# First FFN: down products with the tokens standing, their sums turned by VectorE and read back by GpSimd

## The chip, the cores and the metric

One core of one Trainium2 chip runs the whole kernel. The metric is the device time of one execution in microseconds (us). The engines are TensorE (PE; its weight loads are shown apart as PEld), VectorE (DVE), ScalarE (ACT), GpSimd (POOL) and SyncE (SP). SP and POOL issue the DMAs here: SP's go through hardware queues, POOL's through a software queue.

## The reference

One decoder layer for 512 tokens of 1024 features in float32: an FFN, a mixer of a linear recurrence and windowed attention, and a second FFN, each between two RMS norms, with a residual.

```python
def swiglu(x, w_gu, w_down):
    gate, up = jnp.split(x @ w_gu, 2, axis=-1)
    return (jax.nn.silu(gate) * up) @ w_down
...
x = x + 0.5 * rms_norm(swiglu(rms_norm(x, ffn1_pre_g[l]), ffn1_w_gu[l], ffn1_w_down[l]), ffn1_post_g[l])
```

The hidden width is 2816, or 22 blocks of 128. The case is about the first FFN's `@ w_down`, and about the sum that its post-norm takes over the 1024 features of each token.

## The kernel before

Every product is made of three matmuls on split operands: a high half (`hh`, `whi`, made by ACT's cast) and a low half (`hl`, `wlo`, made by DVE's subtraction), as high by high, low by high and high by low. A matmul has 128 standing columns (its weight load) and up to 512 moving ones.

The first FFN's hidden blocks come in groups (`GROUPS1`): blocks 0 to 3, 4 to 7, 8 to 11, 12 to 15, and 16 to 21.

- **Blocks 0 to 3** (`classic`): gate and up plainly; then the down product of the four blocks, 96 matmuls of 512 columns, chunk by chunk of 128 output features, and each chunk's sum goes to HBM (the loop over `c` with `g == 0`).
- **Groups 4, 8 and 12** run as `octo`: gate and up by a scheme with seven products in place of eight. Their down product (`seven_down`, line 1088) follows while the next octo's forms are made. It has seven steps `a11, s3, a12, s2, s4, a22, s1`, each a product of 256 hidden by 512 outputs by 256 tokens. `by_channels` (L1347) makes a step of 24 matmuls: four blocks of 128 output features stand as weights, 256 tokens move. After six of the steps ACT copies the two PSUM banks to `stage` (L1113), and POOL adds them to the running sums in HBM (`yp_a`, `in_hbm`; accumulating DMAs of L1116). Sums lie there with output features on partitions.
- **Blocks 16 to 21**: an octo of 16 to 19 whose hidden values go through HBM (`h_a`) and come back by SP's reads (`hxa`), then `last_chunks`: blocks 20 and 21 by a smaller scheme (`quad`, L881) whose forms are `u2a` and `g1a`. Then the down product, chunk by chunk: chunks 0 and 1 together, 2, 3 and 4 alone, and chunks 5 to 7 late, in two halves of 256 tokens (`ay`).

At the end each chunk's product is joined with its sum from HBM (`res.chunk` L676, `res.late` L692, both on DVE), squared by ACT, and the squares are added: chunks 0 to 4 by POOL into `acca`, the late halves by DVE into `accb` (L705, L709). PE then takes the mean over features (`rms_r`, L550) of the first 256 tokens, in the middle of the second halves, and of the others after them. The scaled sums are added to x, which POOL reads back from HBM (L1357). `boundary` holds this part.

The next stage's weights (`raw_xl`, `raw_kv`) are loaded by SP through a ring of five `raw` buffers, and `W` hands out units (cast by ACT, low half by DVE) in the order of use. `W.owed` is a list of functions called in place of weight loads.

For the second FFN the seven steps already have tokens as standing operand (`by_tokens`, L1884 to L1886), since its output is wanted with tokens on partitions.

## Time and profile before

| | |
|---|---|
| median of 3 runs | 842.86 us (842.47 to 843.58) |
| the profiled execution | 842.55 us, span 840.8 us |
| PE busy | 832.2 us (99%), 4504 instructions |
| PEld busy | 718.9 us (85%) |
| DVE, ACT, POOL busy | 723.8 (86%), 520.9 (62%), 162.6 us (19%) |
| granted TensorE clock | 0.999 |
| POOL's writes to `yp_a` | 50 of 256 KB, 9.1 us to landing |

A row of the time line has the start, the duration, the engine, the line of the program, the operation, what it writes `<-` reads, the shape and the count; in brackets the idle time before it and what ended it. SPq is SP issuing a DMA: its duration is that of the issue, not of the transfer. A row of the chain of waits has the start, the length, the engine and how many instructions it stands for. Where a part of the span is looked at by itself, the share of busy time over all 840.8 us says little: look at what ends the waits there.

### The profile page before, as it was taken

How to read it: one execution, taken by the hardware profiler on the slowest of the kernel's cores; microseconds unless marked ns; L12 is line 12 of the kernel's file. 1: busy time of each engine (PE TensorE's matmuls, PEld its weight loads, DVE VectorE, ACT ScalarE, POOL GpSimd, SP SyncE). 2: the span in 40 equal slices, each digit the busy share in tenths (PEclk: the TensorE clock that was granted, in tenths of full speed). 3: DMA queues.
4: the chain of work that ended last, by engine and by line, in shares of the span. 5: the costliest groups of instructions: out<-in, count | busy, mean ns of one | idle time of the engine just before them, and what ended most of it. 6: DMA issues, size and time to landing. Idle time of an engine off the chain costs nothing.

```text
span 840.8 us, 12378 instructions
## 1 busy us (share of the span) xinstructions
PE 832.2 (99%) x4504; PEld 718.9 (85%) x4504; DVE 723.8 (86%) x1026; ACT 520.9 (62%) x821; POOL 162.6 (19%) x178
## 2 busy tenths in 40 slices
PE   9999999999999999999999999999999999999996
PEld 8988888988988998987788899888888888888885
DVE  4978999998989965879889589799999899898996
ACT  6646756666666655556797456536758667666562
POOL 2023000140320333304531052002004114032001
PEclk9999999999999999999999999999999999999999
DMA  7249429398595799323511131169439939769842
GB/s 252 77 128 347 135 79 318 80 251 267 123 255 186 167 261 331 93 62 108 157 51 51 51 105 47 50 129 290 179 106 232 317 92 257 253 149 258 305 140 101
DMA packets 123614, 143.73 MB, mean 171 GB/s; under 512 B 23897, under 2 KB 81569, under 8 KB 123041
## 3 DMA queue, kind: packets, MB, share of 16 engines
q1 hardware_dynamic: 109232, 111.86, 42.0%
q0 software_dynamic: 14176, 30.94, 17.0%
q8 instruction: 35, 0.57, 0.3%
q14 instruction: 27, 0.21, 0.1%
q10 hardware_dynamic: 144, 0.13, 0.0%
HBM read 100.45 MB, written 40.89 MB: 168 GB/s over the span
## 4 chain that ended last, share of the span: by engine, by line
PE 96%; DVE 2%; DMA 1%; SPq 0%; issue 0%; ACT 0%; DVEq 0%; ACTq 0%
PE aa L951 10%; PE ab L951 10%; PE db L951 5%; PE da L951 5%; PE yaa L1347 3%; PE bb L951 3%; PE ba L951 3%; PE yda L1347 2%; PE ya L506 2%; PE ya L507 2%; PE ya L508 2%; PE aa L881 1%; PE a_first L1206 1%; PE yab L1884 1%; PE yab L1885 1%; PE yab L1886 1%
## 5 line engine op out<-in xcount | busy, mean ns | idle before, releaser
L1116 POOL DMA_DIRECT2D yp_a<-stage x42 | 36.8, 1064 | 182.6 <-ACT stage L1113 158.8
L1116 POOL DMA_DIRECT2D yp_b<-stage x42 | 36.4, 1084 | 144.3 <-ACT stage L1113 117.8
L506 PE MATMUL ya<-hha,whi_ad 128*128 128x512 f32 x62 | 24.1, 389 | 0.0
L507 PE MATMUL ya<-hla,whi_ad 128*128 128x512 f32 x62 | 24.1, 389 | 0.0
L508 PE MATMUL ya<-hha,wlo_ad 128*128 128x512 f32 x62 | 24.1, 389 | 0.0
L686 POOL TENSOR_TENSOR acca_r<-acca_r,sq_r 128x512 f32<-128x512 f32 x6 | 8.1, 1357 | 61.7 <-ACT sq_r L536 61.7
L1900 POOL DMA_DIRECT2D yp_b<-stage x8 | 4.3, 548 | 67.1 <-ACT stage L1899 67.1
L524 PE MATMUL an<-xh_mx,whi_xl 128*128 128x256 f32 x64 | 15.9, 289 | 0.0
L525 PE MATMUL an<-xh_mx,wlo_xl 128*128 128x256 f32 x64 | 15.5, 283 | 0.0
L2003 POOL TENSOR_TENSOR last<-yp,grow 128x512 f32<-128x512 f32 x3 | 3.9, 1290 | 57.2 <-DVE yp L1993 57.2
L2000 ACT ACTIVATE ysq<-yp 128x512 f32<-128x512 f32 (+1 forms) x8 | 4.8, 606 | 16.2 <-DVE yp L1993 16.2
L506 PE MATMUL gt<-xh_mx,whi_gt 128*128 128x512 f32 x32 | 14.3, 445 | 0.0
L508 PEld LDWEIGHTS ya<-hha,wlo_ad 128*128 128x128 f32 x62 | 11.6, 188 | 2.4
L506 PEld LDWEIGHTS ya<-hha,whi_ad 128*128 128x128 f32 x62 | 11.6, 188 | 2.4
L507 PEld LDWEIGHTS ya<-hla,whi_ad 128*128 128x128 f32 x62 | 11.6, 188 | 2.4
L536 ACT ACTIVATE sq_r<-yp_a 128x256 f32<-128x256 f32 (+1 forms) x10 | 5.0, 502 | 12.9 <-DVE yp_a L676 5.9
L506 PE MATMUL pq<-xh_mx,whi_q 128*128 128x512 f32 x32 | 12.8, 399 | 0.0
L506 PE MATMUL pub<-xh_f,whi_bu 128*128 128x512 f32 x32 | 12.6, 395 | 0.0
L508 PE MATMUL gt<-xh_mx,wlo_gt 128*128 128x512 f32 x32 | 12.6, 394 | 0.0
L506 PE MATMUL pgb<-xh_f,whi_bg 128*128 128x512 f32 x32 | 12.6, 393 | 0.0
L507 PE MATMUL gt<-xl_mx,whi_gt 128*128 128x512 f32 x32 | 12.6, 392 | 0.0
L508 PE MATMUL pgb<-xh_f,wlo_bg 128*128 128x512 f32 x32 | 12.5, 390 | 0.0
(2014 smaller groups left out, 3468.8 us busy)
## 6 DMA issues: line engine op xcount, KB each, us to landing
yp_a<-stage POOLq DMA_DIRECT2D x50, 256.0 KB, 9.1
yp_b<-stage POOLq DMA_DIRECT2D x50, 256.0 KB, 9.0
h_a<-za SPq DMA_DIRECT2D x16, 256.0 KB
hxa<-h_a SPq DMA_DIRECT2D x16, 256.0 KB
h_b<-zb SPq DMA_DIRECT2D x16, 256.0 KB
hxb<-h_b SPq DMA_DIRECT2D x16, 256.0 KB
xn<-in_x SPq DMA_DIRECT2D x8, 256.0 KB
xT_hbm<-xT POOLq DMA_DIRECT2D x2, 1024.0 KB, 9.8
```

Source lines behind the costliest of these rows:

```text
L506: pe.matmul(ps, hi[:, k, :], xh, start=start, stop=False)
L507: pe.matmul(ps, hi[:, k, :], xl, start=False, stop=False)
L508: pe.matmul(ps, lo[:, k, :], xh, start=False, stop=stop)
L524: pe.matmul(ps[:, sl], hi[:, k, :], xh, start=k == 0 and not goes_on, stop=False, skip_group_check=True)
L525: pe.matmul(ps[:, sl], lo[:, k, :], xh, start=False, stop=False, skip_group_check=True)
L881: pe.matmul(o, w[:, k, js], x, start=first and i + j + k == 0, stop=k == 3 and i == 2, skip_group_check=True)
L951: pe.matmul(b[tb], x[:, blk], w[:, k, :], start=first and q + k + j == 0, stop=q + k == 2 and j == 2, skip_group_check=True)
L1116: pool.dma_start(o, st.rearrange("p (a b) -> p a b", a=2) if len(o.shape) == 3 else st, accum_op=ALU.add)
L1206: pe.matmul(banks[j][:, HALF[0]], ws[j][part][:, k, :], n1.xs[k][xpart][:, HALF[0]], start=k == 0 and part == xpart, stop=stop and k == KD ...
L1347: pe.matmul(o, a[:, k, ms], x[:, js], start=first and i + k + m % 2 == 0, stop=k == 1 and i == 2, skip_group_check=True)
L1884: pe.matmul(banks[i], hh[:, js], hi[:, k, :], start=first and k == 0, stop=False, skip_group_check=True)
L1885: pe.matmul(banks[i], hh[:, js], lo[:, k, :], start=False, stop=False, skip_group_check=True)
```

## The change

1. The seven steps of the first FFN's down product take `by_dealt_tokens` in place of `by_channels`: 128 tokens of a hidden block stand, 512 weight columns move, 12 matmuls a step. The hidden halves are kept as four blocks of 64 + 64 tokens in the order in which a later 32x32 turn wants them (`by_blocks`, `dealt`, `in_turn`), and `hxa` comes back in two DMAs in place of four.
2. The sums in HBM are rows: `yr_a`, tokens on partitions, eight pieces of 128x512. The first group's down product (`first_down`) also has tokens standing, in two passes of four banks, with its weights loaded as two raws and made into four units, and the hooks that make the next octo's sums and lows moved with them.
3. The last step (`s1`) of the last octo stays in its two PSUM banks (`hold`), and isn't copied nor added in HBM.
4. At the end of the FFN SP reads the eight row pieces, behind the last weight loads (`W.owed`). DVE turns them in blocks of 32x32 (`turn_sums`), the second half after adding the held banks; SP writes them to `yt_a`, output features on partitions; POOL reads the eight chunks back (`read_sums`).
5. POOL's masks are made earlier, and `decay_factor` moves from the first octo to the second.

```diff
+    def by_token_blocks(o, h, w, k, blk, start, stop):
+        (hh, hl_), (hi, lo) = h, w
+        for j, (x, a) in enumerate(((hh, hi), (hh, lo), (hl_, hi))):
+            pe.matmul(o, x[:, blk], a[:, k, :], start=start and j == 0, stop=stop and j == 2, skip_group_check=True)
+    def by_dealt_tokens(banks, w, h, first):
-    def by_channels(banks, w, h, first):
-        (hi, lo), (hh, hl_) = w, h
-        for m in range(4):
-            o, ms = banks[m // 2][:, HALF[m % 2]], slice(m * P, (m + 1) * P)
+        for i in range(2):
             for k in range(2):
-                js = HALF[k]
-                for i, (a, x) in enumerate(((hi, hh), (hi, hl_), (lo, hh))):
-                    pe.matmul(o, a[:, k, ms], x[:, js], start=first and i + k + m % 2 == 0, stop=k == 1 and i == 2, skip_group_check=True)
+                by_token_blocks(banks[i], h, w, k, slice((2 * i + k) * P, (2 * i + k + 1) * P), first and k == 0, k == 1)
...
+    def read_rows(dh):
+        t = wpool.tile([P, NB * T], F32, tag="raw", name=f"rows_a{dh}", bufs=NRAW)
+        row_sums[dh] = [t[:, tb * T:(tb + 1) * T] for tb in range(NB)]
+        for tb in range(NB):
+            sync.dma_start(row_sums[dh][tb], rows_hbm[tb, dh])
+    def turn_sums(dh):
+        z = wpool.tile([P, NB * T], F32, tag="raw", name="zy1", bufs=NRAW) if dh else wide("zy0")
+        for tb in range(NB):
+            if dh:
+                dve.tensor_add(row_sums[dh][tb], row_sums[dh][tb], held[tb % 2])
+            dve.transpose(z.rearrange("p (j b n) -> p b j n", n=32, b=NB)[:, tb], row_sums[dh][tb].rearrange("p (j n) -> p j n", n=32))
+        for i in range(4):
+            sync.dma_start(turned_hbm[dh][:, i * P:(i + 1) * P].rearrange("(j a) n -> a j n", a=32), z[32 * i:32 * (i + 1)].rearrange("p (j n) -> p j n", n=P))
+    def read_sums(cs):
+        for c in cs:
+            parts[c] = t2k(f"yp_a{c}")
+            pool.dma_start(parts[c], turned_hbm[c // 4][(c % 4) * P:(c % 4 + 1) * P])
...
             if g > 1:
-                seven_down(hid, before, by_channels, lambda half, dh, i: in_hbm[2 * dh + i][:, half], hid.forms, AHEAD - 1)
+                held = seven_down(hid, before, by_dealt_tokens, lambda half, dh, i: rows_hbm[2 * half + i, dh], hid.forms, AHEAD - 1, hold=f1 == FC)[1, 1]
             if f1 == FC:
-                W.owed = [lambda: None] * 2
+                W.owed = [W.load, W.load, lambda: read_rows(0), lambda: read_rows(1)]
+                neg, upf = masks()
...
-            for c in range(5):
-                parts[c] = t2k(f"yp_a{c}")
-                sync.dma_start(in_halves(parts[c]), in_hbm[c // 2][:, :, c % 2])
+        for dh in range(2):
+            turn_sums(dh)
+        dve.tensor_copy(up8f, upf)
+        read_sums(range(4))
```

PE, the first step (`a11`) of the down product of group 4: its first six matmuls before, then after. A row has the line, the bank written, and behind `<-` the moving operand first and the standing one second.

```order
L1347 MATMUL yaa_1627<-hha_1446,whi_adp__1516 128x256
L1347 MATMUL yaa_1627<-hla_1448,whi_adp__1516 128x256
L1347 MATMUL yaa_1627<-hha_1446,wlo_adp__1517 128x256
L1347 MATMUL yaa_1627<-hha_1446,whi_adp__1516 128x256
L1347 MATMUL yaa_1627<-hla_1448,whi_adp__1516 128x256
L1347 MATMUL yaa_1627<-hha_1446,wlo_adp__1517 128x256
```

```order
L1360 MATMUL yaa_1611<-whi_adp__1500,hha_1430 128x512
L1360 MATMUL yaa_1611<-wlo_adp__1501,hha_1430 128x512
L1360 MATMUL yaa_1611<-whi_adp__1500,hla_1432 128x512
L1360 MATMUL yaa_1611<-whi_adp__1500,hha_1430 128x512
L1360 MATMUL yaa_1611<-wlo_adp__1501,hha_1430 128x512
L1360 MATMUL yaa_1611<-whi_adp__1500,hla_1432 128x512
```

Weights and hidden values have changed places, the moving width has doubled, and a step has 12 such rows where it had 24.

SP, at the end of the first FFN, from the last weights of its down product (`raw_ad`) to the first of the next stage, before and after:

```order
L175 DMA raw_ad__3210<-in_ffn_w_down 128x6x256
L175 DMA raw_ad__3281<-in_ffn_w_down 128x6x256
L1380 DMA yp_a_3322<-yp_a_591 128x2x256
L1380 DMA yp_a_3324<-yp_a_591 128x2x256
L1380 DMA yp_a_3326<-yp_a_592 128x2x256
L1380 DMA yp_a_3328<-yp_a_592 128x2x256
L1380 DMA yp_a_3330<-yp_a_593 128x2x256
L1309 DMA gates_raw<-in_w_rg 64x4x64 x2
L1309 DMA gates_raw<-in_w_ig 64x4x64 x2
L175 DMA raw_xl__3349<-in_w_in 128x8x256
L1389 DMA yp_a_3394<-yp_a_593 128x2x256
```

```order
L1376 DMA rows_a_2940<-yr_a_597 128x512
L1376 DMA rows_a_3014<-yr_a_592 128x512
L1376 DMA rows_a_3014<-yr_a_594 128x512
L1376 DMA rows_a_3014<-yr_a_596 128x512
L1376 DMA rows_a_3014<-yr_a_598 128x512
L1385 DMA yt_a_599<-zy_3058 32x16x128 x4
L1385 DMA yt_a_600<-zy_3067 32x16x128 x4
L1332 DMA gates_raw<-in_w_rg 64x4x64 x2
L1332 DMA gates_raw<-in_w_ig 64x4x64 x2
L175 DMA raw_xl__3099<-in_w_in 128x8x256
L175 DMA raw_xl__3192<-in_w_in 128x8x256
L175 DMA raw_kv<-in_w_in 128x8x256
```

The eight reads of ready chunks (the last two of them and raw_xl's second load stand behind the rows shown) have become eight reads of rows (three more stand ahead, behind `raw_ad`) and eight writes of turned sums, all ahead of the gates and of the next weights.

DVE, at the same place, behind the quad's last form, before and after:

```order
L891 TENSOR_TENSOR hla_3077<-g1a_3085,hha_3076 128x2x4x32
L1329 CAST up_590<-upf 128x512
L215 TENSOR_TENSOR wlo_ad_0_3284<-raw_ad__3210,whi_ad_0_3283 128x768
L215 TENSOR_TENSOR wlo_ad_1_3346<-raw_ad__3210,whi_ad_1_3345 128x768
L676 TENSOR_TENSOR yp_a_3322<-ya_3354,yp_a_3322 128x512
L676 TENSOR_TENSOR yp_a_3324<-ya_3355,yp_a_3324 128x512
```

```order
L908 TENSOR_TENSOR hla_2803<-g1a_2811,hha_2802 128x2x4x32
L1383 STREAM_TRANSPOSE zy_3058<-rows_a_2940 128x16x32 x4
L1382 TENSOR_TENSOR rows_a_3014<-rows_a_3014,yaa_2609 128x512
L1383 STREAM_TRANSPOSE zy_3067<-rows_a_3014 128x16x32
L1382 TENSOR_TENSOR rows_a_3014<-rows_a_3014,yaa_2610 128x512
L1383 STREAM_TRANSPOSE zy_3067<-rows_a_3014 128x16x32
L1382 TENSOR_TENSOR rows_a_3014<-rows_a_3014,yaa_2609 128x512
L1383 STREAM_TRANSPOSE zy_3067<-rows_a_3014 128x16x32
L1382 TENSOR_TENSOR rows_a_3014<-rows_a_3014,yaa_2610 128x512
L1383 STREAM_TRANSPOSE zy_3067<-rows_a_3014 128x16x32
L1449 CAST up_590<-upf 128x512
L215 TENSOR_TENSOR wlo_ad_0_3020<-raw_ad__2813,whi_ad_0_3019 128x768
```

Twelve instructions now stand between the last form and the low halves of the weights of chunks 4 to 7; the subtraction of chunk 0 follows two rows further.

## The prediction

> **What bounds the kernel now.** I read the page first: the busy times, then the chain that ended last.

> ```profile
> span 840.8 us, 12378 instructions
> PE 832.2 (99%) x4504; PEld 718.9 (85%) x4504; DVE 723.8 (86%) x1026; ACT 520.9 (62%) x821; POOL 162.6 (19%) x178
> PE 96%; DVE 2%; DMA 1%; SPq 0%; issue 0%; ACT 0%; DVEq 0%; ACTq 0%
> ```

> TensorE (PE) is busy for all but 8.6 us of the span and is 96% of the chain. So there are only two ways to move the time: give PE less to do, or make it wait where it doesn't wait now. The profiled execution took 842.55 us, 1.75 more than its span; the median of the three runs, 842.86, lies 0.31 above it. All sums below are made in the profiled execution, and 0.31 is added at the end. About 0.2% (1.7 us) is what a measurement of this kernel can tell from no change, and the chances are split there.

> Next the chain of waits in order of time, round a down stage of the first FFN, and the table by stretches: its columns are PE busy, weight loads (PEld), DVE, ACT, POOL, granted clock, DMA share, GB/s. The first three stretches are the three down stages of seven steps in the first FFN; the last is the same stage in the second FFN, where the tokens already stand.

> ```profile
> 152.97 2.04 PE aa L951 x9
> 155.01 2.87 PE yaa L1347 x24
> ...
> 172.28 2.88 PE yaa L1347 x24
> 175.16 5.01 PE aa L951 x22
> ```

> ```profile
> 155.01:175.16 20.15, 20.15 (x170) 20.15 (x169) 20.08 (x23) 14.65 (x22) 7.05 (x8) 1.00 0.65 153
> 213.27:233.43 20.16, 20.16 (x170) 20.16 (x169) 19.59 (x22) 14.65 (x22) 6.99 (x8) 1.00 0.66 154
> 271.53:291.69 20.16, 20.16 (x171) 20.16 (x170) 18.50 (x21) 12.47 (x19) 6.72 (x8) 1.00 0.63 142
> 621.92:640.96 19.04, 19.04 (x86) 15.77 (x85) 19.04 (x22) 12.13 (x19) 6.63 (x8) 1.00 0.54 126
> ```

> See two things. A step of 24 matmuls with 256 moving columns takes 2.88 us, 0.120 each, and the weight loads fill the whole stretch: 20.15 of 20.15. In the second FFN the same seven steps are 84 matmuls of 512 columns, 19.04 us, 0.227 each, with 3.3 us of the load path free. The granted clock is 1.00 in all four.

> **The gain.** The first FFN's three stages take the form of the last row: 20.15 + 20.16 + 20.16 - 3 x 19.04 = **3.35 us** less. DVE is full in the fourth row (19.04 of 19.04) and PE still does not wait, so DVE's 20.08 us in the first is no objection: its weights are made steps ahead. [...]

> **The first group.** Its 96 down matmuls keep their number and 512 columns; only the operands change places. Two looser things move: the first weights of the next octo now go ahead of the fourth block's low halves on DVE.

> ```profile
> 72.72 0.69 DVE L659 TENSOR_TENSOR t24l_a<-tb_a,t24h_a 128x512 fp32r<-128x512 f32 x1
> ```

> ```profile
> 78.85 5.44 PE aa L951 x24
> ```

> Those lows end at 73.4 now, and would end near 75 to 76; the first octo product starts at 78.85 and uses the fourth block some 3.6 us into its 24 matmuls. Cover of 6 us: cost zero, and if the cover were gone, at most the 2 us of delay. The strided casts (`by_blocks`, `in_turn`) have the form of the quad's (L891 below, 0.76 for two of 256 columns, against 0.69 for one flat 512): nothing.

> **The end of the FFN.** Here is the price. Today eight chunks come back from HBM long before PE has the products they join. Now rows must be read, turned by DVE, written, and read again by GpSimd, all after the quad's last form. DVE, ACT and SyncE rows of that place now, and PE's:

> ```profile
> 315.53 0.76 DVE L891 TENSOR_TENSOR hla<-g1a,hha 128x256 fp32r<-128x256 f32 x2 [0.47 <-ACT hha L888]
> ...
> 319.39 1.37 DVE L676 TENSOR_TENSOR yp_a<-ya,yp_a 128x512 f32<-128x512 f32 x2 [1.02 <-PE ya L508]
> ...
> 334.64 1.74 DVE L215 TENSOR_TENSOR wlo_xl<-raw_xl__3440,whi_xl 128x1024 fp32r<-128x1024 f32 x1 [0.50 <-ACT whi_xl L210]
> ...
> 339.84 0.43 DVE L709 TENSOR_TENSOR accb_r<-accb_r,sq_r 128x256 f32<-128x256 f32 x1 [0.53 <-ACT sq_r L536]
> ```

> ```profile
> 312.39 0.84 ACT L210 CAST whi_ad<-raw_ad__3210 128x768 fp32r<-128x768 f32 x1 [3.91 <-DMA raw_ad__3210<-in_ffn_w_down]
> ...
> 313.75 0.59 ACT L921 ACTIVATE g1a<-aa 128x512 f32<-128x512 f32 x1
> ...
> 320.75 1.28 ACT L482 ACT_TABLE_LOAD   x1
> ...
> 322.68 0.82 ACT L210 CAST whi_ad<-raw_ad__3281 128x768 fp32r<-128x768 f32 x1
> ```

> ```profile
> 298.37 0.47 SPq L175 DMA_DIRECT2D raw_ad__3210<-in_ffn_w_down  x1
> ...
> 311.03 2.39 SPq L1309 DMA_DIRECT2D gates_raw<-in_w_rg  x2
> 314.27 1.31 SPq L1309 DMA_DIRECT2D gates_raw<-in_w_ig  x2
> ```

> ```profile
> 308.96 2.88 PE aa L881 x24
> 311.85 0.23 PE ya L506
> ...
> 341.99 0.34 PE rms_r L550 x4
> ```

> The residual's mean (L550) is the deadline: it needs the last partial sum (L709), which ends at 340.27, 1.7 us early. With 3.35 us less before it, PE ends the quad at 308.5 and wants that sum at **338.6**. How late the sum comes is worked out hop by hop.

> *Start of the turning.* DVE takes it up after hla of g1a, at 316.29 now. ACT was held there until 312.39 by a load issued at 298.37. Lower end: PE's 308.5 and the 2.5 us from g1a's activation (313.75) to 316.29, so 311.0. Upper end: nothing shifts, 316.3. The load's slot is freed by PE's progress, so it moves with the 3.35; the four accumulating writes that the held step drops (1 MB) relieve the DMA queues somewhat. I take 311.7.

> *Turn, write, land.* Two rows of DVE and SyncE give the same pattern in an octo:

> ```profile
> 159.48 1.30 DVE L961 STREAM_TRANSPOSE za<-g1a 128x512 f32<-128x512 f32 x2
> ```

> ```profile
> 219.07 2.83 SPq L965 DMA_DIRECT2D h_a<-za  x4
> ...
> 224.36 3.27 SPq L1021 DMA_DIRECT2D hxa<-h_a  x4
> ```

> Four turns 2.5, four writes 2.83, and 2.46 more until their reader could be issued (224.36 - 221.90): the first half is in HBM at 319.5.

> *GpSimd's reads.* Software DMAs of 256 KB, from the group's writes, and the times of 1 MB loads:

> ```profile
> L1416 POOL DMA_DIRECT2D yp_a<-stage x8: 682/697/833, 65.5 to 82.8; - x8
> ...
> DMA to landing us min/median/max: 2.5/6.1/8.8
> ```

> ```profile
> L210 ACT CAST whi_bd<-raw_bd x2: 1032/1040/1047, 565.1 to 566.5; 128x1024 fp32r<-128x1024 f32 x2
> ...
> L175 SPq DMA_DIRECT2D raw_bd<-in_ffn_w_down x1: 455/455/455, 559.7 to 559.7; - x1
> ```

> ```profile
> 75.72 1.69 SPq L175 DMA_DIRECT2D raw_ay__901<-in_ffn_w_gu  x2
> ```

> ```profile
> 85.20 1.23 DVE L296 TENSOR_TENSOR raw_ax__862<-raw_ay__901,raw_ax__862 128x1024 f32<-128x1024 f32 x1 [3.12 <-DMA raw_ay__901<-in_ffn_w_gu]
> ```

> A 256 KB read lands 2.5 to 8.8 us after its issue; 4.5, between the least and the median, gives chunk 0 at 324.0. PE has its product by then, so chunk 0's subtraction on DVE now waits for a DMA, and queued behind it are wlo of raw_ad46 (two), the lows of raw_xl and every later sum.

> *The next weights.* raw_xl2's load now takes the buffer of raw_ad46, which is free when DVE has its second low. From chunk 0 (319.39) to the end of that weight's cast (323.50) is 4.1 us on ACT, table load included, and the low adds 0.95: issue at 329.1. A 1 MB load took 5.4 (raw_bd, 559.7 to 565.1) and 9.5 (raw_ay__901, 75.7 to 85.2); with GpSimd's eight reads and raw_xl0 about, 6.5, nearer to the quiet one because those reads are spread over some 10 us: 335.6. Cast 1.04. From the low of raw_xl2 (334.64) to the last sum (340.27) is 5.6. Sum at **342.3**.

> *SyncE's side* agrees. The second half's four sums and four turns take 4.9 more on DVE (319.1), its writes 2.83, the gates 4.55 as now (311.03 to 315.58) and raw_xl0 follows at 326.5; landed at 332 to 333, two casts and lows, chunk 4 and the late halves, some 9.7, end at 342 to 343.

> So PE waits 342.3 - 338.6 = 3.7 us at the mean, once; c5 to c7's second halves follow at their old pace, and x's reload (GpSimd) lands in that wait. Net -3.35 + 3.7 = +0.35, 842.9 for this execution, and 843.2 with the 0.31. The two dropped ACT copies and the fewer hxa issues lie beside PE: nothing.

> **Rivals.**

> *The round trip hides* (faster). For it: the short end of each link, 311.0 + 2.5 + 2.83 + 2.46 + 2.5 = 321.3, then 5.05, a load of 5.4, and 6.65 give 338.4, before 338.6. PE waits for nothing: 842.86 - 3.35 = **839.5**. [...] It decides where the sum comes before 340.2. Against it: the DMA engines are full at this place.

> ```profile
> 309.00:312.00 3.00, 3.00 (x26) 2.96 (x25) 2.97 (x5) 0.00 (x0) 0.00 (x0) 1.00 1.10 234
> ```

> *The hops land as under load* (slower). One mechanism: with the queues full as in that row, GpSimd's reads take their median 6.1 and raw_xl2 its 9.5. That is 1.6 + 3.0 us later: the sum at 346.9, PE waits 8.3, net +5.0, **847.8**; with the turning also at 313.5, 849.6. It decides from a sum at 343.6 on, 1.3 us behind my forecast: the median landing alone suffices.

> [...]

> **How the numbers follow.** The forecast, within 1.7 us of no change: 0.34. The round trip hides by enough: 0.31. Lands late: 0.32; steps don't shorten: 0.03, together 0.35 slower. The likeliest case has 841.2 to 844.5 for its own; the range is 839.4 (all hidden) to 848.5, and leaves out only the last of the loaded case.

> **What would show it.** Steps of 2.72 in the chain at the three stages: the gain. PE's idle before L555's mean (the L550 of now), put down to the sum: the wait; its size says which case. The landing of GpSimd's eight reads, ACT's and DVE's waits for raw_xl: which hop. DVE's first turn before 311 or after 314 would break the start. The prediction falls altogether if PE waits at another place, in the first group for instance.

## The result, and the profile after

The changed kernel takes **854.15 us** (median of four runs, 850.15 to 854.82) against 842.93 for the kernel before on the same chip: 1.0123 times, 95% interval 1.009 to 1.0155. It is slower, and outside the range on record; the forecast was 843.2. The profiled execution took 854.6 us.

The first two lines of the profile's page:

```profile
span 852.5 us, 11869 instructions
PE 834.6 (98%) x4252; PEld 709.1 (83%) x4252; DVE 735.5 (86%) x1034; ACT 519.2 (61%) x815; POOL 159.6 (19%) x182
```

PE has 252 instructions less and yet is busy 2.4 us longer: matmuls got slower somewhere, and PE stood still besides. The 11.7 us between the two spans fall on these places in PE's row (first and last matmul of each part, after less before):

| part | us |
|---|---|
| up to the first group's down product | -0.39 |
| the three stages of seven steps | -2.26 |
| wait ahead of the mean over the first tokens (L555, before L550) | +7.84 |
| the last group's down product and mx's first products (`an`), without that wait | +2.25 |
| all behind it: the mixer, from its first product (`pk`) to its last (`po`) | +4.26 |
| sum | +11.70 |

The first row is no gain of the change: the other versions of the changed kernel begin the octo behind the first group from 0.2 us earlier to 0.4 us later than the kernel before.

**The stages.** The table by stretches, columns as before:

```profile
154.46:174.64 20.18, 20.04 (x86) 15.57 (x84) 20.18 (x25) 12.65 (x20) 5.71 (x7) 1.00 0.44 107
212.72:231.76 19.04, 19.04 (x86) 15.77 (x84) 19.01 (x23) 13.42 (x21) 7.01 (x8) 1.00 0.63 150
269.84:288.88 19.04, 19.04 (x86) 15.77 (x84) 17.27 (x21) 11.08 (x18) 5.35 (x7) 1.00 0.60 135
```

The second and third stage have the forecast 19.04. The first did not shrink, and DVE is full to the last hundredth there. Twenty us earlier in DVE's row stands the decay factor, small operations from 132.79 to 136.26 that the change moved here; the last row is the low half of the step `s4`'s form:

```profile
132.79 0.16 DVE L1297 TENSOR_SCALAR nabs<-cols 128x4 f32<-128x4 f32 x1
...
136.09 0.17 DVE L1317 TENSOR_SCALAR nka<-ka 128x4 f32<-128x4 f32 x1
...
165.88 0.68 DVE L851 TENSOR_TENSOR hls<-s4a,hhs 128x512 fp32r<-128x512 f32 x1
```

The same low half before, and PE's first products of `s4` after:

```profile
162.40 0.68 DVE L834 TENSOR_TENSOR hls<-s4a,hhs 128x512 fp32r<-128x512 f32 x1
```

```profile
165.53 0.50 PE L1360 MATMUL yea<-whi_adt__1594,hhs 128*128 128x512 f32 x1
166.01 0.49 PE L1360 MATMUL yea<-wlo_adt__1595,hhs 128*128 128x512 f32 x1
166.62 0.50 PE L1360 MATMUL yea<-whi_adt__1594,hls 128*128 128x512 f32 x1
```

DVE's work is 3.48 us late here (165.88 against 162.40), and the delay reaches PE in `s4`, whose forms and weights are only just made: its first products start 0.48 and 0.61 us apart, where 0.227 is usual.

**The end of the FFN.** DVE, SyncE, GpSimd, ACT and PE in order of time:

```profile
311.99 2.48 DVE L1383 STREAM_TRANSPOSE zy<-rows_a 128x512 f32<-128x512 f32 x4
...
326.14 0.69 DVE L681 TENSOR_TENSOR yp_a<-ya,yp_a 128x512 f32<-128x512 f32 x1 [4.35 <-DMA yp_a<-yt_a]
328.71 0.69 DVE L681 TENSOR_TENSOR yp_a<-ya,yp_a 128x512 f32<-128x512 f32 x1 [1.88 <-DMA yp_a<-yt_a]
...
346.69 0.42 DVE L714 TENSOR_TENSOR accb_r<-accb_r,sq_r 128x256 f32<-128x256 f32 x1 [0.53 <-ACT sq_r L541]
```

```profile
314.50 8.07 SPq L1385 DMA_DIRECT2D yt_a<-zy  x8
...
327.14 0.60 SPq L175 DMA_DIRECT2D raw_xl__3099<-in_w_in  x1
331.81 0.40 SPq L175 DMA_DIRECT2D raw_xl__3192<-in_w_in  x1
```

```profile
321.36 2.24 POOL L1390 DMA_DIRECT2D yp_a<-yt_a  x4 [21.40 <-PE ya L512]
331.39 2.16 POOL L1390 DMA_DIRECT2D yp_a<-yt_a  x4 [7.79 <-DMA yt_a<-zy]
```

```profile
340.51 1.04 ACT L210 CAST whi_xl<-raw_xl__3192 128x1024 fp32r<-128x1024 f32 x1 [1.92 <-DMA raw_xl__3192<-in_w_in]
```

```profile
347.17 1.01 PE L555 MATMUL rms_r<-mean_d,accb_r 128*128 128x1 f32 x4 [7.84 <-DVE accb_r L714]
```

The turning begins where it was expected. GpSimd's first reads go out 1.9 us later than reckoned (321.4, not 319.5), the second half's at 331.4; raw_xl's second load at 331.8 (329.1), and its cast runs 8.7 us behind that (6.5). The last sum ends at 347.1, not 342.3, and PE stands still for 7.84 us.

**The clock.** The table by stretches of 3.41 us round that wait; look at PE's busy time, the first number behind the comma, and at the granted clock, third from the end:

```profile
338.25:341.66 3.41, 1.08 (x10) 0.88 (x8) 1.38 (x2) 1.39 (x2) 3.31 (x5) 1.00 1.10 402
341.66:345.07 3.41, 0.00 (x0) 0.00 (x0) 2.67 (x4) 0.54 (x2) 0.49 (x1) 0.50 1.02 422
345.07:348.49 3.42, 1.32 (x6) 1.32 (x7) 1.95 (x5) 1.40 (x5) 0.00 (x0) 0.50 1.05 365
348.49:351.90 3.41, 3.41 (x16) 3.23 (x16) 2.31 (x6) 1.43 (x3) 1.29 (x1) 0.50 0.31 92
351.90:355.31 3.41, 3.41 (x30) 3.41 (x30) 3.25 (x9) 2.00 (x5) 1.71 (x2) 1.00 1.02 296
```

PE is idle from 339.3. Some 2.3 us later its clock is halved, and it stays so until 351.9, 4.7 us after the work has begun again: 16 matmuls in a stretch where the next has 30 at full clock. The clock fell behind a stretch of 3.41 us in which PE was idle for 2.33 us (the first row), and rose behind one in which PE never stood still (348.49 to 351.90).

**The mixer.** DVE and GpSimd, before and after (`wlo_gt` are weights' low halves, `xcl` the low half of a conv block), and PE after:

```profile
398.82 1.21 DVE L215 TENSOR_TENSOR wlo_gt<-raw_gt__3993,whi_gt 128x1024 fp32r<-128x1024 f32 x1
399.01 2.19 POOL L1475 TENSOR_TENSOR xcl<-xc,xch 128x512 fp32r<-128x512 f32 x1 [0.90 <-ACT xch L1474]
```

```profile
406.47 1.30 POOL L1529 TENSOR_TENSOR xcl<-xc,xch 128x512 fp32r<-128x512 f32 x1 [0.66 <-ACT xch L1528]
...
406.52 2.33 DVE L215 TENSOR_TENSOR wlo_gt<-raw_gt__3745,whi_gt 128x1024 fp32r<-128x1024 f32 x1
...
410.14 1.70 DVE L1549 TENSOR_TENSOR qT1l<-qT,qT1h 128x512 fp32r<-128x512 f32 x1 [0.42 <-ACT qT1h L1548]
411.76 2.42 DVE L215 TENSOR_TENSOR wlo_gt<-raw_gt__3793,whi_gt 128x1024 fp32r<-128x1024 f32 x1
...
415.47 1.60 DVE L1549 TENSOR_TENSOR qT2l<-qT,qT2h 128x512 fp32r<-128x512 f32 x1 [0.43 <-ACT qT2h L1548]
```

```profile
419.13 0.49 PE L1652 MATMUL cur<-home 64*128 64x128 f32 x4 [1.88 <-DVE home L1542]
```

Where such operations of the two met, one took almost twice its time (2.33 us and not 1.21 at 406.52): the one that started second, as far as the recorded starts tell (at the meeting of 411.76 DVE started 0.03 us ahead of GpSimd and lost all the same). Before, GpSimd lost; now DVE loses four times, 4.3 us over the lone times (1.21 and 0.68), and PE waits 1.88 us for DVE's `home` copy. The clock then falls again:

```profile
416.76:420.17 3.41, 1.53 (x17) 1.13 (x14) 2.80 (x5) 2.42 (x4) 0.25 (x1) 1.00 0.91 262
420.17:423.58 3.41, 3.41 (x10) 2.63 (x9) 3.31 (x6) 1.94 (x6) 1.75 (x2) 0.50 1.00 322
```

A wait of 1.9 us and 3.41 us of work at a granted clock of 0.50, by that row an estimated 1.7 us lost, make 3.6 of the 4.26.

### The profile page after: what moved, and what is told of

Read it like the earlier page. It is cut to its first block, busy times and chain, and to the rows that moved or that the text cites. A ratio compares the mean times of both kernels' runs of the same rounds, so it can differ in the third digit from the quotient of the medians.

```text
span 852.5 us, 11869 instructions
## 1 busy us (share of the span) xinstructions
PE 834.6 (98%) x4252; PEld 709.1 (83%) x4252; DVE 735.5 (86%) x1034; ACT 519.2 (61%) x815; POOL 159.6 (19%) x182
## 4 chain that ended last, share of the span: by engine, by line
PE 46%; DVE 9%; issue 2%; ACT 2%; DMA 1%; SPq 0%; DVEq 0%; ACTq 0%
PE ab L968 10%; PE db L968 4%; PE bb L968 3%; PE yab L1940 1%; PE yab L1938 1%; PE yab L1939 1%; DVE xc L1502 1%; PE mn L529 1%; PE an L529 1%; PE gt L511 1%; PE an L530 1%; PE mn L530 1%; PE mn L536 1%; PE an L536 1%; PE ydb L1940 1%
## 5 line engine op out<-in xcount | busy, mean ns | idle before, releaser
L1139 POOL DMA_DIRECT2D yr_a<-stage x38 | 33.3, 1004 | 183.9 <-ACT stage L1136 157.2
L1139 POOL DMA_DIRECT2D yp_b<-stage x42 | 36.5, 1040 | 144.3 <-ACT stage L1136 118.1
L513 PE MATMUL pq<-xh_mx,wlo_q 128*128 128x512 f32 x32 | 12.5, 390 | 0.0
L512 PE MATMUL pq<-xl_mx,whi_q 128*128 128x512 f32 x32 | 12.5, 390 | 0.0
L513 PE MATMUL pub<-xh_f,wlo_bu 128*128 128x512 f32 x32 | 12.5, 389 | 0.0
L512 PE MATMUL pgb<-xl_f,whi_bg 128*128 128x512 f32 x32 | 12.5, 389 | 0.0
L512 PE MATMUL pub<-xl_f,whi_bu 128*128 128x512 f32 x32 | 12.5, 389 | 0.0
L1360 PE MATMUL ya<-whi_ad,hha 128*128 128x512 f32 x32 | 12.4, 389 | 0.0
L1360 PE MATMUL ya<-wlo_ad,hha 128*128 128x512 f32 x32 | 12.4, 389 | 0.0
```

Source lines behind the costliest of these rows:

```text
L512: pe.matmul(ps, hi[:, k, :], xl, start=False, stop=False)
L513: pe.matmul(ps, lo[:, k, :], xh, start=False, stop=stop)
L1139: pool.dma_start(o, st, accum_op=ALU.add)
L1360: pe.matmul(o, x[:, blk], a[:, k, :], start=start and j == 0, stop=stop and j == 2, skip_group_check=True)
```

## The experiments

All are timed beside the kernel before, which took 842.65 to 843.47 there. The theory after the result: the wait ahead of the mean, with the clock that falls behind it, is the loss at the end of the FFN, and it has two chains, GpSimd's chunks and raw_xl's loads; the decay factor costs the first stage its gain; the mixer's loss is a matter of which engine comes first by tenths of a us. The rival: the longer first stage and the mixer have causes of their own in the new form of the steps.

| run | median us | waits of PE, end of FFN | mixer, `pk` to `po` |
|---|---|---|---|
| before | 842.9 | none | 80.8 |
| after | 854.15 | 7.8 | 85.1 |
| e1_decay | 852.98 | 8.4 | 84.9 |
| e2_free | 850.96 | 5.3 | 84.7 |
| e3_spin | 850.03 | filled | 80.9 |
| e4_nudge (on before) | 844.81 | none | 81.2 |
| e5_early | 854.12 | 0.6 + 9.0 | 80.9 |
| e6_early_free | 855.44 | 4.8 + 2.3 | 85.1 |
| e7_early_decay | 854.47 | 0.8 + 7.5 | 84.6 |
| e8_before_decay (on before) | 844.04 | none | 81.3 |
| e9_loads | 851.41 | 6.1 | 83.1 |
| e10_loads_free | 844.15 | 0.8 | 83.4 |
| e11_loads_decay | 851.13 | 7.4 | 80.9 |
| e12_pool_late | 852.63 | 7.6 | 82.2 |
| e13_turn_early | 851.00 | 1.5 + 1.1 + 5.0 | 81.2 |
| e14_turn_mid | 850.41 | 6.4 | 81.2 |
| e15_rows_first | 850.15 | 4.1 | 85.1 |
| e16_rows_spin | 845.63 | filled + 0.6 | 83.8 |

Waits and mixer are those of the profiled execution of each, the median is over all its runs.

**e1_decay and e8_before_decay: the decay factor.** The changed kernel with it back in the first octo (e1, shown), and the kernel before with it in the second (e8, the same lines the other way):

```diff
-            beside = hid.seven_forms_of(before, h_hbm[before], dealt_halves=True) if g > 1 else {}
-            if g == 2:
-                beside[2] = [lambda: decay.append(decay_factor())]
+            beside = hid.seven_forms_of(before, h_hbm[before], dealt_halves=True) if g > 1 else {2: [lambda: decay.append(decay_factor())]}
```

> The changed kernel with the decay factor (some 15 small DVE instructions, 3.4 us, and two table loads of ACT) put back into the first octo. Theory: in the changed kernel these instructions stand at 133 to 136 us, in front of a down stage in which DVE has no slack, and cost the first of the three stages its gain: it took 20.2 us and not 19.04. So here that stage takes 19.04 to 19.1 us and the quad ends 1.1 us earlier; the round trip of the sums is set by DMAs and moves less than that, so the time falls by 0 to 1.1 us against the changed kernel. Rival: the stage is slow because DVE is full there anyhow (20.1 of 20.15 us before); it stays at 20.2 us.

> The kernel before with one part of the change alone: the decay factor computed in the second octo instead of the first. If its 3.5 us on DVE push the weights of the first stage past their use, as read from the changed kernel, the first stage takes 1 us or more over its 20.15 and the time is 843.9 or more; if the steps of before, 1.1 us a stage longer, leave enough cover, the stage stays at 20.15 and the time at 842.9.

The first stage of e1, then of e8:

```profile
155.22:174.26 19.04, 19.04 (x86) 15.77 (x84) 19.01 (x23) 13.27 (x21) 7.06 (x8) 1.00 0.61 149
```

```profile
154.83:175.61 20.78, 20.40 (x170) 20.19 (x168) 20.78 (x25) 12.99 (x21) 6.37 (x8) 1.00 0.46 109
```

Undone, it gives the full 19.04; alone on the kernel before it costs 0.63 us in the stage, and 844.04 us against 843.47 (ratio 1.0008, 0.9999 to 1.0018), which the time alone would not tell from no change. So the moved decay factor, not the form of the steps, kept 1.1 of the gain. In e1 the wait behind grew from 7.8 to 8.4: a gain ahead of a wait whose end does not move is given back there in part.

**e2_free: the turned sums.** Turns and writes run, but GpSimd reads from the row sums, which have long been there, so that the sums added are not the turned ones (the same holds for e6 and e10):

```diff
-            pool.dma_start(parts[c], turned_hbm[c // 4][(c % 4) * P:(c % 4 + 1) * P])
+            pool.dma_start(parts[c], rows_hbm[c % 4, c // 4])
```

> The changed kernel with GpSimd's eight chunk reads taken from the row sums in HBM instead of the turned ones: the turns and their writes still run, but nothing waits for them; the sums that are added are the wrong ones. Theory: the wait of 7.8 us at the mean is the round trip; without it PE waits less than 1 us there, the granted clock stays at 1.00, and the time is 840.6 (842.9 less the 2.3 us that the steps gained), 844.9 if VectorE and GpSimd still collide in the mixer. Rival: the wait comes from the loads of the next weights behind full DMA queues; then PE still waits over 4 us and the time stays above 846.

PE's waits, in the view that sums them (total, times, longest):

```profile
PE rms_r L555 <- DVE accb_r L714: 5.3, 1, 5.3
```

The chunks are not the only chain. raw_xl's loads still stood on SyncE behind eight writes and the gates.

**e5_early, e6_early_free, e7_early_decay: the loads ahead, spoilt.** raw_xl's first load and the gates were put ahead of the writes; for room, the second half was turned into the other wide buffer:

```diff
-        z = wpool.tile([P, NB * T], F32, tag="raw", name="zy1", bufs=NRAW) if dh else wide("zy0")
+        z = wide(f"zy{dh}")
...
+        W.load()
+        W.owed = [W.load, W.load, lambda: None]
+        load_gates()
```

> The changed kernel with the next stage's first loads taken out of the round trip's way: zy1 lies in the other wide buffer instead of a raw one, raw_xl's first load and the gates are issued by SyncE ahead of the eight yt_a writes, and raw_xl's second load takes the buffer of chunk 4 and 5's weights, behind the writes. Theory A (raw_xl's loads behind the writes and gates set the end): its second load is issued near 322.6 instead of 331.8, and the wait ahead of the mean (7.8 us) falls below 3, to where the chunks' reads set it; with a wait below 2 us the clock stays at 1.00: 844 to 848. Theory B (GpSimd's reads of the chunks set the end): chunks 5 to 7 still land at 335 to 340, the wait stays at 6 or more and the time at 852 or more.

> The same, and GpSimd reads the chunks from the row sums, which are ready (so that turns and writes run but nothing waits for them; the sums read are not turned and so are the wrong ones). With both chains loose, the wait ahead of the mean is below 1 us whichever of the two sets it alone, and the clock stays at 1.00 there: 854.2 - 7.8 - 2.3 = 844 with the mixer's collision of DVE and GpSimd, 840 without it. If the wait stays above 4 us, a third chain is there that neither theory names.

> The early loads and the decay factor back in the first octo: 1.1 us below the early loads alone if the parts add up (843 to 847), with all three stages of seven steps at 19.04 us; the same as the early loads alone if the decay's place only shifts when PE gets to the wait.

These runs tell nothing of the two chains: that buffer was the first half's own. DVE in e5 (in e6 it waits 8.11 us at the same row):

```profile
321.49 0.71 DVE L1383 STREAM_TRANSPOSE zy<-rows_a 128x512 f32<-128x512 f32 x1 [5.65 <-DMA yt_a<-zy]
```

The second half's turns waited for the first half's writes to leave the buffer, and everything behind them on DVE with them.

**e9_loads, e10_loads_free, e11_loads_decay: the loads ahead.** As e5, e6 and e7, but turned into the first half's row buffer, which only DVE reads:

```diff
-        z = wpool.tile([P, NB * T], F32, tag="raw", name="zy1", bufs=NRAW) if dh else wide("zy0")
+        z = row_sums["tile"] if dh else wide("zy0")
```

> The early loads again, without the wait that spoilt them: the second half is now turned into the first half's row buffer, which DVE alone has read, so that no turn waits for a write. SyncE issues raw_xl's first load and the gates ahead of the yt_a writes; raw_xl's second load stands behind the writes. Theory A (raw_xl's loads behind writes and gates set the end): the second load is issued near 322.6 instead of 331.8, the wait ahead of the mean falls from 7.8 us to below 3 and the time to 844 to 848. Theory B (GpSimd's reads of chunks 4 to 7 set the end, landing at 335 to 340): the wait stays at 5 or more, the time at 851 or more.

> The same with GpSimd reading the chunks from the row sums, so that nothing waits for turns and writes (the sums read are not turned, so the wrong ones). With both chains loose the wait ahead of the mean is below 1.5 us and the clock stays at 1.00 there: 844 with the mixer's collision, 840 without. A wait of 4 us or more means a third chain, DVE's own order for instance.

> The early loads without the spoiling wait, and the decay factor back in the first octo, the version that should come nearest to the kernel before or beat it: 1.1 us below the early loads alone by the steps (all three stages 19.04). Beats before (below 842) only if the wait ahead of the mean is below 2 us and the mixer runs without the collision; with either in the way 845 to 850.

In e9, SyncE's second load of raw_xl (331.81 in the changed kernel), GpSimd's second reads, and PE's wait:

```profile
323.12 1.15 SPq L175 DMA_DIRECT2D raw_xl__3100<-in_w_in  x1
```

```profile
331.36 2.16 POOL L1391 DMA_DIRECT2D yp_a<-yt_a  x4 [7.46 <-DMA yt_a<-rows_a]
```

```profile
PE rms_r L555 <- DVE accb_r L714: 6.1, 1, 6.1
```

And the mean in e10:

```profile
340.56 0.61 PE L555 MATMUL rms_r<-mean_d,accb_r 128*128 128x1 f32 x4 [0.76 <-DVE accb_r L714]
```

With the loads ahead the wait is 6.1, with free reads 5.3, with both 0.8. **Each of the two chains alone holds the mean for most of the time that both do**, and neither theory A nor B alone was right. With both loose the time is 844.15, 1.0016 times before (0.9999 to 1.0032), with a mixer that still waits in the profiled execution: the whole loss at the end of the FFN is the round trip and what it pushes back. e11's first stage has its 1.1 us, and its wait is 1.2 us longer than e9's.

**e3_spin: the clock.** The changed kernel with 36 dummy 128x128 products on PE ahead of the mean:

```diff
+            for i in range(SPIN if self.name == "r10" else 0):
+                pe.matmul(ps[:, P:2 * P], ident, ident, start=True, stop=True)
```

> The changed kernel with 36 idle 128x128 matmuls by PE (into an unused part of the mean's bank) ahead of the first mean, about 7.7 us at full clock. Theory: the granted clock drops to 0.5 because PE stands still for 7.8 us, and costs 2.25 us after the wait; with PE busy it stays at 1.00 from 340 to 352 us, and the time falls by 2 to 2.5 us (852 with the later collision in the mixer, 848 without). Rival: the clock drops for another reason (power, DMA load), stays at 0.5 there, and the time stays or grows.

```profile
348.00:350.00 2.00, 2.00 (x16) 1.85 (x16) 1.74 (x6) 1.30 (x4) 0.60 (x1) 1.00 1.09 332
```

The clock stays at 1.00; from the down product's first matmul to the end of mx's first products it takes 66.3 us where after took 68.4, with the last sum ready at 346.8 (347.1). That is 2.1 of the 2.25. Two of its four runs took 848.1 and 848.3, two 851.7 and 852.2; the profiled one is of the first pair and has no wait in the mixer.

**e4_nudge and e12_pool_late: the mixer.** Two operations of 128x4 on DVE in the kernel before; and in the changed kernel 128 columns done twice more ahead of GpSimd's third and fourth xcl:

```diff
+        if name == "qT0":
+            for _ in range(2):
+                dve.tensor_scalar(late_by, nka, 1.0, None, op0=ALU.mult)
```

```diff
+        for _ in range(2 if ci >= 2 else 0):
+            pool.tensor_sub(xl[:, :P], xcs[ci][:, :P], xh.bitcast(F32)[:, :P])
```

> The kernel before the change, with two 128x4 instructions (0.4 us) added on DVE between the copy and the split of the first query block. Theory: in the mixer it is decided by 0.2 us whether DVE's low half of a gate weight or GpSimd's subtraction starts first; the one that comes second takes twice as long, and after the changed order DVE is always second. With the nudge DVE's instructions there take 2.3 us where they took 1.2, PE waits some 1.9 us for a copied query block, its clock halves for some 3 us, and the time is 846 to 847.5. Rival: the order there doesn't matter, and 0.4 us of DVE work is hidden: 842.9 within 0.5.

> The changed kernel with GpSimd held up by some tenths of a us in the mixer: ahead of the third and the fourth xcl it does the first 128 columns twice over, so that VectorE's wlo_gt starts ahead of it, as in the kernel before. If the order in which the two start decides (the one that comes second takes about twice its time), wlo_gt takes 1.2 us again where it took 2.3 and 2.4, PE does not wait 1.9 us for the home copy, the clock does not fall at 420, and the time is 4.3 us less than the changed kernel: about 850. If the mixer's loss has another cause, the wait of 1.9 us stays and the time with it, 854.

0.36 us of work made two groups of e4's ten runs: five at 843.06 to 843.30, five at 846.31 to 847.42. So the kernel before has a loss of this size in it, and a few tenths of a us call it up; that the slower five have the mixer's wait is inferred, since none of them was profiled. The profiled execution took 843.06, and DVE loses the first meeting there:

```profile
399.22 2.30 DVE L215 TENSOR_TENSOR wlo_gt<-raw_gt__3993,whi_gt 128x1024 fp32r<-128x1024 f32 x1
```

PE did not wait: losing that meeting is not enough. In e12, GpSimd and DVE at the first meeting, and DVE at the next:

```profile
406.86 1.87 POOL L1530 TENSOR_TENSOR xcl<-xc,xch 128x128 fp32r<-128x128 f32 x2 [0.66 <-ACT xch L1528]
```

```profile
406.90 1.50 DVE L215 TENSOR_TENSOR wlo_gt<-raw_gt__3745,whi_gt 128x1024 fp32r<-128x1024 f32 x1
...
410.70 2.31 DVE L215 TENSOR_TENSOR wlo_gt<-raw_gt__3793,whi_gt 128x1024 fp32r<-128x1024 f32 x1
```

GpSimd still started 0.04 us ahead, its extra columns took 0.94 us each beside DVE and not tenths, and DVE lost 3.1 us over four operations. PE's wait for `home` was gone and the clock up; the mixer took 82.2, so 2.9 of 4.3 us came back. The simple theory, that the first of these meetings decides, falls: PE waited in the nine profiles in which DVE lost the same four operations, some 4.2 to 4.4 us in sum, and not where it lost 3.1 or less. What sets off the row is open. In these nine, all of the changed kernel, the wait is 1.8 to 2.0 us, and the mixer takes 83.1 to 83.8 where the clock stayed up and 84.6 to 85.1 where it fell; five other versions, with the same new steps, take 80.9 to 81.2 without it (e12 apart), so the new form of the steps is not the cause by itself.

**e13_turn_early, e14_turn_mid, e15_rows_first, e16_rows_spin: an earlier start.** All with the early loads and the decay factor in the first octo. The first half is turned in the quad; in e15 the second half's row reads also go ahead of the first half's writes; e16 adds 16 dummy products. The line of e13 is shown; e14 has 5 for the 4, and e15 and e16 call `W.owed.pop(0)()`, the row reads, ahead of `turn_sums(0)` there:

```diff
-            xs = hid.last_chunks(f0, h_hbm[f0], {})
+            xs = hid.last_chunks(f0, h_hbm[f0], {4: lambda: turn_sums(0)})
```

> The early loads and the decay factor in the first octo, and the first half turned during the quad, behind the second low half of raw_ad's first weights, near 302 instead of 312; its writes stand ahead of the second half's row reads on SyncE. If both chains end the wait, as the four runs with free reads and early loads say, and the chunk chain is as long as its hops, moving its start up by 6 to 9 us brings chunks 4 to 7 to 331 to 334 and the wait ahead of the mean below 2 us: 854.2 - 7.8 - 2.3 - 1.1 = 843 with the mixer's collision, 839 without, which beats the kernel before. If DVE stalls on the rows (they are issued at 298 to 303), the quad's last forms come late, PE waits at the down product's third or fifth block and the time is 847 or more.

> The same with the first half turned one step later in the quad, behind u2a, near 308: no stall on the rows, the start moved up by 4 us only. The wait ahead of the mean between 2 and 5 us, the clock low behind it when it is over 2: 842 to 849.

> The first half turned in the quad behind u2a, the row reads of the second half issued ahead of the first half's writes (in the two runs before they stood behind them and landed at 317, so that the second half's turning began no earlier than with the turns behind the quad), raw_xl's first load and the gates between the two groups of writes. If the start of each half decides, the second half is turned from 314 on, written by 320, read back by 333 and the wait ahead of the mean is 1 to 3 us: 842 to 847. If the hops under load decide (the last of the second half's writes landed near 330.8 in every version so far), the second reads are still issued near 331, the wait stays at 5 to 6 and the time at 850.

> The same with 16 dummy 128x128 products (3.6 us) on PE ahead of the mean of the first tokens, so that PE stands still less than 2 us there and the clock stays up. If the granted clock costs what the changed kernel's rows say, 1.5 to 2.3 us below the run without them where that run waits over 3 us; the same time or slightly more where it doesn't.

DVE in e13, then GpSimd's reads in e14 and in e15:

```profile
307.62 2.51 DVE L1384 STREAM_TRANSPOSE zy<-rows_a 128x512 f32<-128x512 f32 x4 [6.37 <-DMA rows_a<-yr_a]
```

```profile
317.10 2.24 POOL L1391 DMA_DIRECT2D yp_a<-yt_a  x4 [18.70 <-PE ya L513]
331.38 2.16 POOL L1391 DMA_DIRECT2D yp_a<-yt_a  x4 [12.03 <-PE ay L513]
```

```profile
317.02 2.24 POOL L1391 DMA_DIRECT2D yp_a<-yt_a  x4 [18.89 <-PE ya L513]
328.76 2.16 POOL L1391 DMA_DIRECT2D yp_a<-yt_a  x4 [9.51 <-PE ya L513]
```

The rows land only near 307.6, so e13's early place is a stall. The PE in the brackets is what came last by time, no cause: in e13 the second reads went out at 331.25, ahead of ya's end at 332.2; they wait for the four writes as in the changed kernel. In e14 the first half's reads go 4 us earlier and the second half's not at all, because its rows had moved behind the first half's writes. e15 takes that away: second reads at 328.8, wait 4.1. So the start counts, but only 2.6 us of its gain arrive: the second half's writes are issued from 319.1 to 322.2 and read from 328.8 on, six us and more of landing under load. e16 is the best version with the right sums, 845.63 (1.0039, 1.0017 to 1.0061): the dummies hold the clock, five of its ten runs lie between 843.99 and 844.79, and the others between 846.46 and 852.04; the profiled one, 847.03, has the mixer's wait, what the slower ones have was not seen. None beats the kernel before.

## Why the prediction was wrong

The sum on record was +0.35 us, the profiled execution's span grew by 11.70. Of the 11.35 between them 1.09 are gain that did not come, 4.14 a wait that was put too short, 2.25 the slow clock behind it and 4.26 the mixer, less the 0.39 by which this execution was ahead early on. The place and the kind of the wait were forecast rightly; the steps that failed are its hops, taken as quiet, the two terms put at nothing, and the slack of the first stage.

- **The gain, 3.35 us:** the steps did shorten to 2.72, and two stages to 19.04. 2.26 came. The failing step is the decay factor, which the change's list named and the sum left out, under "DVE is full in the fourth row and PE still does not wait, so DVE's 20.08 us in the first is no objection: its weights are made steps ahead". A full engine took 3.5 us more work, and in the first stage the weights of `s4` were made in that step, not steps ahead.
- **The first group, zero:** right. Its products take the same time; the octo behind it starts 0.39 us earlier, as they do, which is the scatter of the start.
- **The wait, 3.7 us:** the mechanism, the place and the deadline (338.6; it was 339.3) were right, the hops were too short. Start 311.7 (312.0) and the chunk reads' 4.5 (4.7 for chunk 0) were good; the writes' landing of 2.46 was about 4.0 by the first reads' issue, chunk 1 came 2.6 behind chunk 0 and held DVE again, raw_xl's second load landed in about 8.7, not 6.5. "Quiet" landings were taken for a place whose DMA row read 1.10, and where the prediction's own rows had ACT waiting until 312.39 for a load issued at 298.37, 14.0 us. The 2.5 to 8.8 us given for a read of 256 KB are from a row of GpSimd's writes; its eight reads took 3.6 to 7.4 here. The rival of loaded hops had the sum at 346.9 and the wait at 8.3: 347.1 and 7.84 it was. That is in part luck: it put 6.1 us on chunk 0's read, which took 4.7, and left the writes' landing at 2.46. SyncE's side, said only to agree, turned out to be a second chain that holds the mean by itself.
- **No term for the clock, 2.25 us:** every row of before that it shows has 1.00, and behind the start of the program PE's longest wait there is 0.3 us. A wait in a kernel without any was priced at its length alone.
- **No term for the mixer, 4.26 us:** "c5 to c7's second halves follow at their old pace" ended the sum at the FFN. What follows was taken to shift as a whole; DVE and GpSimd meet by tenths of a us there. The prediction's own sign, that it falls altogether if PE waits at another place, came true twice: in the first stage and at `home`.
- **The steps don't shorten**, given 0.03, is refuted by the second and third stage, 19.04 us each.

## What to carry to other kernels

When a round trip is put in front of a deadline, price its hops as that place's DMA row shows them, and also everything queued behind it on the issuing engine: here each of the two alone held the end for most of the wait. The wait on PE cost its length and the slow clock behind it (7.84 and 2.25 us here), and dummy work there bought the second part back (2.1 us). Small operations moved onto an engine that is full in one stage can lengthen that stage, whatever the engine's mean: 3.5 us of them cost 1.1 us here and 0.6 on the kernel before. What a stop of 1.8 to 2.0 us cost in clock here depended on how it fell on the grid described below.

## What the hardware showed unasked

```profile
344.73:348.14 3.41, 1.62 (x14) 1.41 (x12) 1.57 (x5) 1.25 (x3) 0.88 (x1) 1.00 1.00 416
348.14:351.55 3.41, 2.75 (x19) 2.53 (x20) 2.80 (x8) 1.68 (x6) 0.85 (x1) 1.00 0.97 294
```

- So the same wait of 1.8 to 2.0 us at the same instruction lowered the clock in the six profiles of nine in which it fell into one window, and left it at 1.00 in the three (e9, e10 and e16) in which a window's edge divided it. The least idle time that cost the clock, 1.84 us, is a little over half a window.
- 256 KB writes in pieces of 512 bytes, issued beside reads and a 1 MB load: in e15 the second half's four were issued from 319.13 to 322.20, and GpSimd's reads of them went out at 328.76, 6.6 us behind. In the changed kernel the last of the second half's writes took 9.5 us (321.34 to 330.84), and GpSimd's second reads follow it at 331.39.
